# Moving a layer norm's running sums and other elementwise work off GpSimd

## The chip, the cores and the metric

The kernel runs on one core of one Trainium2 chip. The metric is the device time of one execution in microseconds (us); for a kernel that was run several times it is the median of the runs. The core's engines work side by side and wait for each other through semaphores: TensorE (PE, matrix products; its weight loads are listed apart as PEld), VectorE (DVE, elementwise work), ScalarE (ACT, one-input functions), GpSimd (POOL, elementwise work here) and SyncE (SP, which issues the transfers). Operands lie in the on-chip memory SBUF; products are accumulated in PSUM.

## The reference

The kernel computes a small encoder trunk: two layers over 512 tokens of 1024 features, fp32 in and out. Each layer is three sub-layers, each followed by a layer norm:

```python
for i in range(DEPTH):                       # DEPTH = 2
    mods = (cond @ ada_w[i] + ada_b[i]).reshape(b, N_SUB, 3, D_MODEL)
    gate = lambda s: (1 + mods[:, s, 2])[:, None, :]
    y = swiglu(modulate(x, mods[:, 0]), ffn_w_gate[i, 0], ffn_w_up[i, 0], ffn_w_down[i, 0])
    x = layer_norm(ALPHA * x + 0.5 * gate(0) * y, ln_g[i, 0], ln_b[i, 0])
    u = modulate(x, mods[:, 1])
    y = mamba2_bidir(u, ...) if i % 2 == 0 else diff_attention(u, ...)
    x = layer_norm(ALPHA * x + gate(1) * y, ln_g[i, 1], ln_b[i, 1])
    y = swiglu(modulate(x, mods[:, 2]), ffn_w_gate[i, 1], ffn_w_up[i, 1], ffn_w_down[i, 1])
    x = layer_norm(ALPHA * x + 0.5 * gate(2) * y, ln_g[i, 2], ln_b[i, 2])
```

`modulate` is x * (1 + scale) + shift, with scale and shift columns of `mods`; ALPHA is 4 ** 0.25. So the program is: FFN (n=0), a Mamba mixer (n=1), FFN (n=2), FFN (n=3), attention (n=4), FFN (n=5), with a layer norm behind each.

## The kernel before

Everything is kept transposed: the 1024 features are 8 tiles of 128 partitions, with the 512 tokens along the free axis. The residual `res` is 8 such tiles of 128x512. A product in fp32 accuracy is made of three fast products: a weight w is split into a high part `wh` (rounded by ACT) and a low part `wl = w - wh` (subtracted by DVE), an activation likewise into `uh` and `ul`, and `mm3` (line 162) issues wh·uh, wh·ul and wl·uh. Weights stream through a ring of four load buffers `raw`, loaded by SP (line 93). The first units of a sub-layer are split in two halves of 512 columns, whose parts are named `wah` (ACT, line 110) and `wal` (line 112); in the program's first units both `wal` halves are on DVE, afterwards the first half is on GpSimd and the second on DVE.

Beside the products runs the stream of the modulation: `ada_unit` (line 180) loads 512 KB of `ada_w` into the same ring and multiplies and accumulates it with the condition vector on DVE, 144 times in all.

**The startup loop** (lines 1027 and on) runs over the 8 feature tiles d. For each it makes two modulation units, two columns shift and scale (line 193, DVE), from them `uh` and `uf` (line 1045, ACT), `ul = uf - uh` (line 1047, GpSimd for d = 0, DVE for the others), scales the residual tile by ALPHA in place (line 1051, GpSimd) and splits one weight unit (lines 110 and 112, for d = 6 and 7 lines 119 and 120). Order is forced in two places: the `wah` and `wal` of a unit are made to come behind `uh` and `ul` of their tile.

**The down projection and the layer norm.** A sub-layer's last product is made unit by unit, unit d giving output tile d. `add_res` (line 371, DVE) adds it, gated, from PSUM into the residual, and `LN.feed` follows: ACT squares the tile (line 288), and two running sums over the tiles d are kept, `sc` of the values (line 292) and `ss` of the squares (line 293). For the tiles that are fed whole both sums are on GpSimd. The last KEEP tiles (4 in an FFN, 6 behind the mixer and the attention) are fed in two halves of 256 tokens; there `sc` is on DVE and `ss` on GpSimd, but for the very last tile, whose `ss` is on DVE too.

Before the first feed, `LN.start` takes a rough mean from tile 0 (ACT line 271, PE line 272, ACT line 274: `m0`) and subtracts it from all 8 residual tiles (line 277): tiles 0 to 5 on DVE, 6 and 7 on GpSimd. Once a half is complete, `stats` takes the mean of `sc` by a product with a constant matrix (line 299, PE), the sums of `sc` and `ss` per token (line 303, PE), a few small DVE steps (lines 308 to 313), a power on GpSimd (line 317) and a broadcast on PE (line 249); DVE subtracts the mean (line 321), and `normalize` multiplies (line 347, DVE) and makes the next sub-layer's `uh` and `ul` (line 349 ACT, line 350 DVE).

Four accumulators of 512 columns (`acc`) take turns, so a product whose accumulator `add_res` has not emptied waits for DVE.

**What sets the order.** A scheduler puts each engine's instructions in an order from the data they need; on an engine they then run strictly one after another. Work with no hurry is kept in a list `later`: in all sub-layers but the first the scaling of the residual waits there.

Of the kernel before, what the change touches and what calls it, by code (L numbers as in the profile page):

```python
# [17 lines left out]
KT = D // P  # L18
# [28 lines left out]
def hybrid_trunk(tc, xT, cb, par, cst, adaw, wgu, wdn0, wdn1, wdn2, wdt, win, wso, wqk, wv, wao, dist_in, dtp, lam_in, out):  # L47
# [47 lines left out]

    extra = [None]
    behind = []
    first_split = [True]
    first_ln = [None]
    turn = [0]  # L100

    def split(raw, where=None):

        n = raw.shape[-1]
        if where == "a":
            hi, lo = [], []
            for o in range(0, n, T):
                r = raw[:, o : o + T]
                h, l = big(F32R, "wah"), big(F32R, "wal")
                x = nc.scalar.activation(h, r, AF.Copy)  # L110
                eng = nc.vector if first_split[0] or o else nc.gpsimd
                y = eng.tensor_tensor(out=l, in0=r, in1=h.bitcast(F32), op=ALU.subtract)  # L112
                for a, b in zip((x, y), behind):
                    tc.add_manual_dep(a.ins, b.ins.name, NOSYNC, reason="inputs before weights")
                hi.append(h)
                lo.append(l)
            return [(hi[c // T][:, c % T : c % T + P], lo[c // T][:, c % T : c % T + P]) for c in range(0, n, P)]
        hi, lo = ring()
        nc.scalar.activation(hi[:, :n], raw, AF.Copy)  # L119
        nc.vector.tensor_tensor(out=lo[:, :n], in0=raw, in1=hi[:, :n].bitcast(F32), op=ALU.subtract)  # L120
        return Unit(hi, lo, n)
# [138 lines left out]
    class LN:  # L260
# [6 lines left out]
        def start(self):  # L267

            pm = acc("ln")
            z0 = tp.tile([P, T], F32R, tag="t", name="z0")  # L270
            nc.scalar.activation(z0, res[0], AF.Copy)
            nc.tensor.matmul(pm, lhsT=onesn, rhs=z0, start=True, stop=True)
            m0 = ap.tile([P, T], F32, tag="l", name="m0", bufs=3)
            nc.scalar.activation(m0, pm, AF.Copy)
            for d in range(KT):
                eng = nc.gpsimd if d >= 6 else nc.vector
                eng.tensor_tensor(out=res[d], in0=res[d], in1=m0, op=ALU.subtract)  # L277
            self.sc = ap.tile([P, T], F32, tag="l", name="sc", bufs=3)
            self.ss = ap.tile([P, T], F32, tag="l", name="ss", bufs=3)

        def feed(self, d, a, b, late=False):
            z = res[d][:, a:b]
            if d == 0:
                self.start()
                nc.scalar.activation(self.ss[:, a:b], z, AF.Square)
                return
            sq = sp.tile([P, T], F32, tag="sq", name="sq")
            nc.scalar.activation(sq[:, a:b], z, AF.Square)
            c0 = res[0] if d == 1 else self.sc
            e0 = nc.vector if late else nc.gpsimd  # L290
            e1 = nc.vector if late and d == KT - 1 else nc.gpsimd
            e0.tensor_tensor(out=self.sc[:, a:b], in0=c0[:, a:b], in1=z, op=ALU.add)
            e1.tensor_tensor(out=self.ss[:, a:b], in0=self.ss[:, a:b], in1=sq[:, a:b], op=ALU.add)

        def stats(self, a, b):
            n, m = self.n, (b - a) // P
# [91 lines left out]
    def down_units(n, u, units, last, KEEP=4):  # L388


        ln = LN(n) if last else None
        keep = []
        for ld in units:
            for d, w in ld():
                if last and d >= KT - KEEP:
                    keep.append((d, w))
                    continue
                pd = acc()
                proj(pd, w, u)
                add_res(d, pd, n, 0, T)  # L400
                if last:
                    ln.feed(d, 0, T)
            yield
        if last:
            rbs = []
            for a, b in HALVES:
                for d, w in keep:
                    pd = acc()
                    proj(pd, w, u, cols=((a, b),))
                    add_res(d, pd, n, a, b)  # L410
                    ln.feed(d, a, b, late=True)
                if rbs:
                    ln.normalize(*HALVES[0], rbs[0])
                rbs.append(ln.stats(a, b))
            ln.normalize(*HALVES[1], rbs[1])
            next_u[0] = ln.u
            ln.residual()
# [616 lines left out]
    for d in range(KT):  # L1034
# [8 lines left out]
        hl = tuple(ap.tile([P, T], F32R, tag="u", name=x, bufs=2 * KT) for x in ("uh", "ul"))  # L1043
        for o in (hl[0], uf):
            x = nc.scalar.activation(o, res[d], AF.Identity, bias=shift[0][:, d : d + 1], scale=onep[0][:, d : d + 1])
        eng = nc.gpsimd if d == 0 else nc.vector
        y = eng.tensor_tensor(out=hl[1], in0=uf, in1=hl[0].bitcast(F32), op=ALU.subtract)  # L1047
        behind[:] = (x, y) if d else (x,)
        first_ln[0] = y
        up.append(hl)  # L1050
        nc.gpsimd.tensor_scalar(out=res[d], in0=res[d], scalar1=ALPHA, scalar2=None, op0=ALU.mult)
        ks.append(split(load(wgu[0, d // 2, d % 2]), "a" if d < 6 else None))
        behind.clear()
    nc.sync.dma_start(csts, cst[:, : 2 * P].rearrange("p (j q) -> p j q", j=2))
    first_split[0] = False
    behind.clear()
    next_u[0] = up
    st0 = ada_stream(0, range(16, 72))
# [111 lines left out]
```

## Time and profile before

| | |
|---|---|
| runs | 2229.15, 2225.82, 2225.81 us; median 2225.82 us |
| profiled execution | 2227.95 us, of which the span of the trace is 2226.2 us |
| busy: PE, DVE, ACT, POOL | 2161.8, 1697.3, 1055.2, 273.4 us |
| startup loop | 0 to about 62 us |
| layer norms n = 0 to 5, from the first whole-tile feed on | about 350–402, 806–862, 1163–1215, 1525–1580, 1826–1862, 2177–2226 us |
| mean granted TensorE clock | 0.991 of full speed |

A row of a timeline gives the start in us, how long it took, engine, line, operation, the tiles written and read, the shape, and in square brackets the idle time of that engine just before it with what ended it. A row of a group gives line, engine, operation, tiles, shape and count, then the sum of busy time in us and the mean in ns, then the idle time in front of the group. A row of a window gives the window, its length and for PE, PEld, DVE, ACT and POOL the busy time with the number of instructions, then the granted clock, the transfer engines' busy share and GB/s. Instructions of one engine overlap by some tens of ns at their ends, so the price of one in a row of many is the distance of two starts, a little less than its listed duration.

### The profile page before, as it was taken

To read this page: it belongs to the slowest core of one execution; us is meant where nothing else is said; L and a number is where in the kernel's file an instruction comes from. 1 tells how busy PE (TensorE), PEld (TensorE's weight loads), DVE (VectorE), ACT (ScalarE), POOL (GpSimd) and SP (SyncE) were. 2 spreads that over 40 slices of the span, in tenths; PEclk is the share of its full clock that TensorE was granted. 3 is DMA by queue.
4 is the path that set the end of the run, shared out by engine and by line. 5 is a ranking of instruction groups with operands and counts; after the bars stand their busy time and mean duration, and the time that the engine had idled before them with its cause. 6 is when DMAs were issued, how large, how long until landed. Compare 5 with 4: busy or idle time off the path is not lost.

```text
span 2226.2 us, 33653 instructions
## 1 busy us (share of the span) xinstructions
PE 2161.8 (97%) x13030; PEld 1862.6 (84%) x13030; DVE 1697.3 (76%) x2850; ACT 1055.2 (47%) x1758; POOL 273.4 (12%) x332
## 2 busy tenths in 40 slices
PE   7999999999999989999999999999999999999998
PEld 5788888866777679889898989899877778989897
DVE  6865568556766689989888998897766679959696
ACT  4422234757656537434355534344755556425253
POOL 2000003035332330000003000003000012000003
PEclk9999999999999999999999999999999999999999
DMA  8865562375445423545542273733211122323231
GB/s 300 283 210 175 181 200 80 96 184 150 136 132 156 119 70 107 193 156 184 166 133 92 92 253 103 238 106 122 68 57 52 53 67 67 115 75 116 84 117 46
DMA packets 88545, 296.97 MB, mean 133 GB/s; under 512 B 9536, under 2 KB 12992, under 8 KB 88384
## 3 DMA queue, kind: packets, MB, share of 16 engines
q1 hardware_dynamic: 88384, 294.81, 41.8%
q8 instruction: 102, 1.67, 0.3%
q14 instruction: 59, 0.48, 0.1%
HBM read 289.53 MB, written 5.24 MB: 132 GB/s over the span
## 4 chain that ended last, share of the span: by engine, by line
PE 48%; DVE 9%; issue 4%; ACT 3%; DMA 2%; POOL 1%; POOLq 0%; ACTq 0%; DVEq 0%; SPq 0%
PE acc L162 38%; PE mid L162 6%; DVE wl L120 1%; DMA raw<-in_wdn 1%; PE mid L938 1%; DVE raw L464 1%; PE ln L162 1%; DVE wl L455 1%; DVE raw L180 1%; DVE lo L150 1%; PE ln L249 1%; DMA raw<-in_adaw 1%; ACT wh L119 1%; DVE resid L277 1%; DVE resid L371 0%
## 5 line engine op out<-in xcount | busy, mean ns | idle before, releaser
L162 PE MATMUL acc<-hi,wh 128*128 128x512 f32 (+1 forms) x1488 | 506.0, 341 | 9.8 <-DVE resid L371 6.7
L162 PE MATMUL acc<-hi,wl 128*128 128x512 f32 (+1 forms) x1488 | 505.9, 340 | 1.1 <-DVE wl L455 1.1
L162 PE MATMUL acc<-lo,wh 128*128 128x512 f32 (+1 forms) x1488 | 504.9, 339 | 0.0
L162 PE MATMUL acc<-uh,wh 128*128 128x512 f32 (+1 forms) x1256 | 441.6, 352 | 0.3 <-ACT wh L119 0.3
L162 PE MATMUL acc<-ul,wh 128*128 128x512 f32 (+1 forms) x1256 | 439.5, 350 | 0.2 <-DVE ul L1047 0.2
L162 PE MATMUL acc<-uh,wl 128*128 128x512 f32 (+1 forms) x1256 | 438.2, 349 | 0.8 <-DVE wl L120 0.8
L119 ACT ACTIVATE wh<-raw 128x1024 fp32r<-128x1024 f32 (+1 forms) x234 | 238.6, 1025 | 392.3 <-PE acc L162 199.1
L120 DVE TENSOR_TENSOR wl<-raw,wh 128x1024 fp32r<-128x1024 f32 (+1 forms) x234 | 281.2, 1202 | 81.1 <-ACT wh L119 71.3
L162 PEld LDWEIGHTS acc<-hi,wh 128*128 128x128 f32 x1488 | 283.8, 191 | 46.2 <-DVE resid L371 6.5
L162 PEld LDWEIGHTS acc<-hi,wl 128*128 128x128 f32 x1488 | 284.1, 191 | 32.2 <-DVE wl L455 1.5
L162 PEld LDWEIGHTS acc<-lo,wh 128*128 128x128 f32 x1488 | 283.9, 191 | 31.0 <-DVE lo L150 1.0
L162 PEld LDWEIGHTS acc<-uh,wh 128*128 128x128 f32 x1256 | 237.4, 189 | 40.2 <-issue 9.2
L454 ACT ACTIVATE wh<-raw 128x1024 fp32r<-128x1024 f32 x162 | 170.8, 1059 | 207.5 <-DVE raw L464 105.2
L162 PEld LDWEIGHTS acc<-uh,wl 128*128 128x128 f32 x1256 | 237.6, 189 | 35.0 <-issue 3.9
L162 PEld LDWEIGHTS acc<-ul,wh 128*128 128x128 f32 x1256 | 237.8, 189 | 33.7 <-issue 4.4
L180 DVE SCALAR_TENSOR_TENSOR raw<-raw,cond 128x1024 f32<-128x1024 f32 x144 | 176.9, 1235 | 55.8 <-DMA raw<-in_adaw 55.4
L455 DVE TENSOR_TENSOR wl<-raw,wh 128x1024 fp32r<-128x1024 f32 x162 | 196.9, 1219 | 27.1 <-ACT wh L454 26.1
L371 DVE SCALAR_TENSOR_TENSOR resid<-acc,gv,resid 128x512 f32<-128x512 f32 (+1 forms) x172 | 113.0, 659 | 78.5 <-PE acc L162 78.2
L464 DVE TENSOR_TENSOR raw<-raw 128x512 f32<-128x512 f32 x216 | 148.1, 689 | 4.4
L112 POOL TENSOR_TENSOR wal<-raw,wah 128x512 fp32r<-128x512 f32 x13 | 19.7, 1517 | 951.7 <-ACT wah L110 655.5
L162 PE MATMUL mid<-uh,wh 128*128 128x256 f32 (+2 forms) x332 | 94.7, 286 | 0.9 <-DVE up L496 0.9
L162 PE MATMUL mid<-uh,wl 128*128 128x256 f32 (+2 forms) x332 | 93.9, 283 | 0.0
(269 smaller groups left out, 3824.8 us busy)
## 6 DMA issues: line engine op xcount, KB each, us to landing
raw<-in_wgu SPq DMA_DIRECT2D x176, 512.0 KB, 3.9
raw<-in_adaw SPq DMA_DIRECT2D x144, 512.0 KB, 4.6
raw<-in_wdn SPq DMA_DIRECT2D x64, 448.0 KB, 3.7
raw<-in_win SPq DMA_DIRECT2D x40, 512.0 KB, 3.6
raw<-in_wdn SPq DMA_DIRECT2D x32, 512.0 KB, 4.5
rw<-scr SPq DMA_DIRECT2D x32, 512.0 KB, 5.4
ch<-scr SPq DMA_DIRECT2D x32, 256.0 KB, 3.5
raw<-in_wso SPq DMA_DIRECT2D x16, 512.0 KB, 3.5
```

Source lines behind the costliest of these rows:

```text
L119: nc.scalar.activation(hi[:, :n], raw, AF.Copy)
L120: nc.vector.tensor_tensor(out=lo[:, :n], in0=raw, in1=hi[:, :n].bitcast(F32), op=ALU.subtract)
L150: y = nc.vector.tensor_tensor(out=lo, in0=src, in1=hi.bitcast(F32), op=ALU.subtract)
L162: last = nc.tensor.matmul(o, lhsT=a, rhs=b, start=start and j == 0, stop=j == n - 1, skip_group_check=not start)
L180: nc.vector.scalar_tensor_tensor(out=raw, in0=raw, scalar=1.0, in1=cond, op0=ALU.mult, op1=ALU.mult, accum_out=mods[l][:, j : j + 1],)
L249: nc.tensor.matmul(o[:, j * P : (j + 1) * P], lhsT=cols[:, j : j + 1].broadcast_to([P, P]), rhs=ident, start=True, stop=True)
L277: eng.tensor_tensor(out=res[d], in0=res[d], in1=m0, op=ALU.subtract)
L371: nc.vector.scalar_tensor_tensor(out=res[d][:, a:b], in0=pd[:, a:b], scalar=gvec[n][:, d : d + 1], in1=res[d][:, a:b], op0=ALU.mult, op1=A ...
L454: nc.scalar.activation(x[0], r, AF.Copy)
L455: nc.vector.tensor_tensor(out=x[1], in0=r, in1=x[0].bitcast(F32), op=ALU.subtract)
L464: nc.vector.tensor_tensor(out=o, in0=x, in1=y, op=ALU.add)
L938: nc.tensor.matmul(ss[m], lhsT=a[r, c], rhs=b[r, :], start=j == 0, stop=j == 2)
```

## The change

All running sums, all eight subtractions of the rough mean, all `wal` halves and the `ul` of tile 0 are issued to DVE; the scaling of the residual by ALPHA in the startup loop is an ACT instruction that is put on the list `later`. GpSimd keeps the small powers (lines 243 and 317) and two steps of the mixer (lines 763 and 777).

```diff
@@ split
                 x = nc.scalar.activation(h, r, AF.Copy)
-                eng = nc.vector if first_split[0] or o else nc.gpsimd
-                y = eng.tensor_tensor(out=l, in0=r, in1=h.bitcast(F32), op=ALU.subtract)
+                y = nc.vector.tensor_tensor(out=l, in0=r, in1=h.bitcast(F32), op=ALU.subtract)
@@ LN.start
             for d in range(KT):
-                eng = nc.gpsimd if d >= 6 else nc.vector
-                eng.tensor_tensor(out=res[d], in0=res[d], in1=m0, op=ALU.subtract)
+                nc.vector.tensor_tensor(out=res[d], in0=res[d], in1=m0, op=ALU.subtract)
@@ LN.feed
-        def feed(self, d, a, b, late=False):
+        def feed(self, d, a, b):
...
             c0 = res[0] if d == 1 else self.sc
-            e0 = nc.vector if late else nc.gpsimd
-            e1 = nc.vector if late and d == KT - 1 else nc.gpsimd
-            e0.tensor_tensor(out=self.sc[:, a:b], in0=c0[:, a:b], in1=z, op=ALU.add)
-            e1.tensor_tensor(out=self.ss[:, a:b], in0=self.ss[:, a:b], in1=sq[:, a:b], op=ALU.add)
+            nc.vector.tensor_tensor(out=self.sc[:, a:b], in0=c0[:, a:b], in1=z, op=ALU.add)
+            nc.vector.tensor_tensor(out=self.ss[:, a:b], in0=self.ss[:, a:b], in1=sq[:, a:b], op=ALU.add)
@@ the startup loop
-        eng = nc.gpsimd if d == 0 else nc.vector
-        y = eng.tensor_tensor(out=hl[1], in0=uf, in1=hl[0].bitcast(F32), op=ALU.subtract)
+        y = nc.vector.tensor_tensor(out=hl[1], in0=uf, in1=hl[0].bitcast(F32), op=ALU.subtract)
...
-        nc.gpsimd.tensor_scalar(out=res[d], in0=res[d], scalar1=ALPHA, scalar2=None, op0=ALU.mult)
+        later.append(lambda d=d: nc.scalar.activation(res[d], res[d], AF.Copy, scale=ALPHA))
```

The line numbers fall by 1 to 6 with it: line 112 is line 110 afterwards, 110 is 109, 180 is 178, 277 is 274, 292 and 293 are 287 and 288, 299 and 303 are 294 and 298, 371 is 366, 1045 and 1047 are 1040 and 1041, and the scaling, 1051, is 1045.

Three places show how the instructions stand. The first is ACT in the startup loop, at the first two tiles (`uh`, `uf`: the modulated input and its high part; `wah`: a weight's high part). Before:

```order
L1045 ACTIVATE uh<-resid,sh_93,sc_94 128x512
L1045 ACTIVATE uf<-resid,sh_93,sc_94 128x512
L110 ACTIVATE wah<-raw 128x512 x2
L1045 ACTIVATE uh<-resid,sh_93,sc_94 128x512
L1045 ACTIVATE uf<-resid,sh_93,sc_94 128x512
```

Now:

```order
L1040 ACTIVATE uh<-resid,sh_93,sc_94 128x512
L1040 ACTIVATE uf<-resid,sh_93,sc_94 128x512
L109 ACTIVATE wah<-raw 128x512
L1045 ACTIVATE resid<-resid 128x512
L109 ACTIVATE wah<-raw 128x512
L1040 ACTIVATE uh<-resid,sh_93,sc_94 128x512
L1040 ACTIVATE uf<-resid,sh_93,sc_94 128x512
```

Though it is put on the list `later`, the scaling stands inside the loop, between the two high parts of each weight unit.

The second place is DVE in the norm behind the FFN n = 2, from the subtraction of the rough mean on (`acc`: the accumulators that line 371 empties; `wl`, `wal`: low weight parts; `raw`, `mods1`: a modulation unit). Before:

```order
L277 TENSOR_TENSOR resid_88<-resid_88,m0_10724 128x512 x6
L371 SCALAR_TENSOR_TENSOR resid_88<-acc_10743,gv2_2543,resid_88 128x512
L120 TENSOR_TENSOR wl_10857<-raw_10854,wh_10856 128x896
L112 TENSOR_TENSOR wal_11253<-raw_11246,wah_11252 128x512
L371 SCALAR_TENSOR_TENSOR resid_88<-acc_10776,gv2_2543,resid_88 128x512
L180 SCALAR_TENSOR_TENSOR raw_11380,mods1_87<-raw_11380,cond_73 128x1024
L120 TENSOR_TENSOR wl_11386<-raw_11383,wh_11385 128x1024
L180 SCALAR_TENSOR_TENSOR raw_11513,mods1_87<-raw_11513,cond_73 128x1024
L371 SCALAR_TENSOR_TENSOR resid_88<-acc_10809,gv2_2543,resid_88 128x512
```

Now:

```order
L274 TENSOR_TENSOR resid_88<-resid_88,m0_10724 128x512 x8
L366 SCALAR_TENSOR_TENSOR resid_88<-acc_10743,gv2_2543,resid_88 128x512
L366 SCALAR_TENSOR_TENSOR resid_88<-acc_10776,gv2_2543,resid_88 128x512
L287 TENSOR_TENSOR sc_10734<-resid_88 128x512
L288 TENSOR_TENSOR ss_10735<-ss_10735,sq_10766 128x512
L287 TENSOR_TENSOR sc_10734<-sc_10734,resid_88 128x512
L288 TENSOR_TENSOR ss_10735<-ss_10735,sq_10799 128x512
L118 TENSOR_TENSOR wl_10857<-raw_10854,wh_10856 128x896
L110 TENSOR_TENSOR wal_11249<-raw_11246,wah_11248 128x512
L366 SCALAR_TENSOR_TENSOR resid_88<-acc_10809,gv2_2543,resid_88 128x512
```

The subtractions are eight, the sums of the whole tiles stand on DVE in pairs, and the weight split and the modulation units come behind them.

The third place is PE in the norm behind the mixer (n = 1), at the statistics of its second half (`acc_7141`: the last down unit; `acc_7315` and the others with `uh_7159`: the next FFN's first products; `sc`, `ss`: the running sums). Before:

```order
L162 MATMUL acc_7141<-hi_6773,wl_6915 128x256
L162 MATMUL acc_7315<-uh_7159,wah_7287 128x256
L162 MATMUL acc_7364<-uh_7159,wah_7297 128x256
L162 MATMUL acc_7448<-uh_7159,wah_7307 128x256
L162 MATMUL acc_7497<-uh_7159,wh_7444 128x256
L299 MATMUL mid_7216<-sc_6879,onesd_89 128x256
L303 MATMUL ln_7215<-invd_78,sc_6879 128x1 x2
L303 MATMUL ln_7215<-invd_78,ss_6880 128x1 x2
L162 MATMUL acc_7315<-ul_7160,wah_7287 128x256
```

Now:

```order
L160 MATMUL acc_7141<-hi_6773,wl_6915 128x256
L294 MATMUL mid_7216<-sc_6879,onesd_89 128x256
L298 MATMUL ln_7215<-invd_78,sc_6879 128x1 x2
L298 MATMUL ln_7215<-invd_78,ss_6880 128x1 x2
L160 MATMUL acc_7315<-uh_7159,wah_7287 128x256
L160 MATMUL acc_7315<-ul_7160,wah_7287 128x256
L160 MATMUL acc_7315<-uh_7159,wal_7288 128x256
```

The four products of the next FFN that stood ahead of the statistics stand behind them. The norm behind the attention (n = 4) moves in the same way.

4 lines of the change are left out of this document (1 added, 3 removed).

## The prediction

> **What bounds the kernel now.** The page's first part comes first, then the waits of PE.
>
> ```profile
> PE 2161.8 (97%) x13030; PEld 1862.6 (84%) x13030; DVE 1697.3 (76%) x2850; ACT 1055.2 (47%) x1758; POOL 273.4 (12%) x332
> PE acc L162 <- ACT wah L110: 11.5, 1, 11.5
> PE acc L162 <- DVE resid L371: 6.7, 3, 3.1
> PE mid L299 <- DVE sc L292: 6.3, 4, 3.6
> ```
>
> PE fills 97% of the span of 2226.2 us; 64.4 us are left in which it stands still. An edit of elementwise work can only shorten these and the stretches in which PE runs at a lower clock. 11.5 us are the start (one wait); of the rest the largest are DVE's `add_res` and DVE's running sum in the layer norms. So the stages in which PE waits for DVE have to be found and priced one by one; the total of DVE says little.
>
> **What moves.** The groups by shape, first of GpSimd (busy us, mean ns), then the like ones of DVE:
>
> ```profile
> L293 POOL TENSOR_TENSOR ss<-ss,sq 128x256 f32<-128x256 f32 x44 | 34.1, 775 | 42.1 <-ACT sq L288 40.5
> L293 POOL TENSOR_TENSOR ss<-ss,sq 128x512 f32<-128x512 f32 x14 | 20.9, 1494 | 0.0
> L277 POOL TENSOR_TENSOR resid<-resid,m 128x512 f32<-128x512 f32 x12 | 20.5, 1731 | 318.1 <-ACT m L274 316.6 <-PE acc L162 1.5
> L112 POOL TENSOR_TENSOR wal<-raw,wah 128x512 fp32r<-128x512 f32 x13 | 19.7, 1517 | 951.7 <-ACT wah L110 655.5 <-PE ln L272 295.5 <-DVE wal L112 0.6
> L292 POOL TENSOR_TENSOR sc<-resid 128x512 f32<-128x512 f32 x6 | 12.8, 2137 | 18.6 <-DVE resid L371 18.6
> L292 POOL TENSOR_TENSOR sc<-sc,resid 128x512 f32<-128x512 f32 x8 | 11.8, 1474 | 1.9 <-DVE resid L371 1.9
> L277 DVE TENSOR_TENSOR resid<-resid,m 128x512 f32<-128x512 f32 x36 | 38.6, 1138 | 4.1 <-ACT m L274 4.1
> L112 DVE TENSOR_TENSOR wal<-raw,wah 128x512 fp32r<-128x512 f32 x25 | 26.8, 1074 | 3.2 <-ACT wah L110 3.2
> L292 DVE TENSOR_TENSOR sc<-sc,resid 128x256 f32<-128x256 f32 x56 | 32.2, 575 | 6.8 <-POOL sc L292 6.3
> L321 DVE TENSOR_TENSOR resid<-resid,mid 128x256 f32<-128x256 f32 x96 | 36.0, 412 | 1.8 <-PE mid L299 1.8
> ```
>
> The last row is DVE's price for 256 columns without GpSimd beside it, 412 ns; for 512 it is 680 (the `wal` at 33.50, in the next fence). In a row of several I take 0.33 and 0.60 us, the distance of two starts (33.50 to 34.10; for 256 less the same 0.08). Taken over are 40 instructions of 512 columns from the L293, L277 and L292 rows (14 + 12 + 6 + 8), 13 `wal` and one `ul`: 54 x 0.60 + 44 x 0.33 = 47 us. In return DVE's own operations with both inputs in SBUF, which before stood beside GpSimd, become cheaper: (1138 − 680) x 36 = 16.5, (1074 − 680) x 25 = 9.9, (575 − 412) x 56 = 9.1, 35 us in three rows, some more in the weight splits beside them. DVE ends about 5 to 12 us busier, so at about 1705; ACT takes 8 scalings of 0.6. The total is nearly even, so where the work lies decides.
>
> **A. The startup loop, −3 us.** One round (d = 3), and the rows that stand around it:
>
> ```profile
> 28.97 0.16 DVE L193 SCALAR_TENSOR_TENSOR sc<-mods,pars 128x1 f32<-128x1 f32 x1
> 29.17 0.82 ACT L1045 ACTIVATE uh<-resid,sh,sc 128x512 fp32r<-128x512 f32 x1 [3.82 <-DVE sc L193]
> 30.72 0.69 DVE L1047 TENSOR_TENSOR ul<-uf,uh 128x512 fp32r<-128x512 f32 x1 [1.59 <-ACT uf L1045]
> 30.77 1.99 POOL L1051 TENSOR_SCALAR resid<-resid 128x512 f32<-128x512 f32 x1 [4.39 <-ACT uf L1045]
> 31.33 1.10 DVE L112 TENSOR_TENSOR wal<-raw,wah 128x512 fp32r<-128x512 f32 x1
> 32.36 1.21 DVE L180 SCALAR_TENSOR_TENSOR raw<-raw,cond 128x1024 f32<-128x1024 f32 x1
> 33.50 0.68 DVE L112 TENSOR_TENSOR wal<-raw,wah 128x512 fp32r<-128x512 f32 x1
> 34.10 1.21 DVE L180 SCALAR_TENSOR_TENSOR raw<-raw,cond 128x1024 f32<-128x1024 f32 x1
> 35.36 0.16 DVE L193 SCALAR_TENSOR_TENSOR sc<-mods,pars 128x1 f32<-128x1 f32 x1
> 31.91 0.40 PE L162 MATMUL acc<-uh,wah 128*128 128x512 f32 x1
> 32.48 0.49 PE L162 MATMUL acc<-uh,wal 128*128 128x512 f32 x1 [0.17 <-DVE wal L112]
> 32.82 0.39 PE L162 MATMUL acc<-ul,wah 128*128 128x512 f32 x1
> 49.74 1.23 DVE L180 SCALAR_TENSOR_TENSOR raw<-raw,cond 128x1024 f32<-128x1024 f32 x1 [0.32 <-DMA raw<-in_adaw]
> ```
>
> DVE's round is 35.36 − 28.97 = 6.39 us. The `wal` beside GpSimd's scaling takes 32.36 − 31.33 = 1.03, the one without it 0.60: 0.43 a round, in five rounds 2.1. In the first round DVE has a `wal` pair, `ul` and the scaling of GpSimd at once, worth about another 1 us, and the two last tiles 0.4 more: DVE's loop could end 3.5 us sooner. PE follows only as far as it waits: starts at 31.91, 32.48 and 32.82 instead of 0.23 apart, 0.45 lost in a round, with like losses in the other rounds, about 4 us in all. Against it stand the transfers, for which DVE waits already at 49.74. Bounds −0.5 and −4; I take −3, near the rows of DVE. ACT's scaling lies between two `wah` and so 0.6 before the second of these; its `wal` stands one modulation unit later on DVE, and ACT has 3.82 us idle in a round. Without that cover it would cost up to 0.6 x 8 = 4.8.
>
> **B. The norm behind FFN n = 2, −4.5 us.**
>
> ```profile
> 1168.01 3.52 POOL L277 TENSOR_TENSOR resid<-resid,m 128x512 f32<-128x512 f32 x2 [0.88 <-ACT m L274]
> 1168.61 6.99 DVE L277 TENSOR_TENSOR resid<-resid,m 128x512 f32<-128x512 f32 x6
> 1186.49 0.36 PE L162 MATMUL acc<-hi,wh 128*128 128x256 f32 x1 [0.62 <-DVE resid L371]
> 1194.06 1.19 PE L299 MATMUL mid<-sc,onesd 128*128 128x256 f32 x2 [3.65 <-DVE sc L292]
> 1196.00:1198.00 2.00, 2.00 (x10) 2.00 (x11) 1.22 (x7) 0.00 (x0) 0.17 (x1) 0.50 0.00 0
> ```
>
> Six subtractions take 6.99 us on DVE beside two on GpSimd; all eight alone are 8 x 0.60 = 4.8. What follows on DVE is late by that, runs beside GpSimd's sums, and PE stands 3.65 us before the statistics. From there the clock is 0.50 until about 1200.7: of 6.7 us half, 3.3, are lost. So 0.62 + 3.65 + 3.3 = 7.6 us are there. Afterwards DVE has per half unit an `add_res` (0.40), two sums (0.66) and for most a modulation unit or a split (1.14): 2.2 us, against about 2.5 of PE. DVE keeps up, but behind the last product it still has these 2.2, of which PE covers about 1 with ten products of the next unit: a wait of up to 1.3. I take 7.6 − 1.3 and half of the clock's loss as staying: −4.5. Bounds −3 (the clock falls all the same) and −6.5.
>
> **C and D. The norms behind mixer and attention, −1.5 and −2.5 us.**
>
> ```profile
> 816.89 0.39 PE L162 MATMUL acc<-hi,wh 128*128 128x256 f32 x1 [2.92 <-DVE resid L371]
> 818.00:820.00 2.00, 2.00 (x12) 1.95 (x12) 1.58 (x3) 0.42 (x1) 2.00 (x2) 0.57 0.51 141
> 822.34 0.47 DVE L371 SCALAR_TENSOR_TENSOR resid<-acc,gv,resid 128x256 f32<-128x256 f32 x1
> 822.73 0.56 DVE L292 TENSOR_TENSOR sc<-sc,resid 128x256 f32<-128x256 f32 x1
> 828.00:830.00 2.00, 1.73 (x11) 1.43 (x9) 2.00 (x7) 0.00 (x0) 1.45 (x2) 0.63 0.01 4
> 825.81 0.67 PE L299 MATMUL mid<-sc,onesd 128*128 128x256 f32 x2 [0.74 <-DVE sc L292]
> 1838.97 0.58 PE L162 MATMUL acc<-hi,wh 128*128 128x256 f32 x1 [3.14 <-DVE resid L371]
> ```
>
> Here PE waits 2.92 and 3.14 us for the first `add_res` behind the subtractions, and runs for 3.3 us at 0.57. Eight subtractions of 0.60 instead of 6.3 us bring this `add_res` 1.4 sooner; but behind it a split and two whole sums (1.14 + 1.2) now stand ahead of the next ones, which gives back about 1.2. What is won is the clock (about 1.7) and the 0.74 before the statistics. In the second half the statistics of PE stand directly behind the last product, with no `uh` products ahead; DVE must first do `add_res` and two sums for one or two half units, 1.06 each (0.39, as 822.34 to 822.73, and twice 0.33): 1.1 to 2.1 lost, and about 1.2 when the next products start before ACT has more than one `uh` ready (an estimate: ACT made `uh` and `uf` at 0.72 each in the startup, two such tiles of half the width and their like). Sum for C: −0.2 − 1.7 − 0.7 − 1.6 (a second such stretch of slow clock, from 828) + 2.1 + 1.2 − 0.6 (waits that fall away) = −1.5, bounds −4 and +2. D has the same rows and one more gain: a slowed `wal` ahead of the rough mean, 1.1: −2.5, bounds −5 and +1.
>
> The clock fell behind a wait of 2.92 us, and again (0.63 from 828) behind 0.74 and smaller ones; so I count waits of 1 to 2 us as able to cost it. By the Trainium skill, "TensorE: Matmul & The Clock Gate", section "Part 1: The HAM clock gate", it falls after an idle window of about 3.4 us. By that, what is left of the waits would cost no clock in B, C and D, the rival "more" below; the 0.63 at 828 speaks against it.
>
> **E. The other norms, 0.** There PE has no gap though DVE is slowed in the same way:
>
> ```profile
> 360.00:380.00 20.00, 20.00 (x147) 18.86 (x146) 15.16 (x28) 5.13 (x10) 13.95 (x11) 1.00 0.32 106
> ```
>
> DVE is busy 15.2 of 20 us; some 8 us more for a norm, half of it given back, still fit, so PE's work hides them. Without that cover it would be up to 4 us a norm.
>
> **Sum:** −3 − 4.5 − 1.5 − 2.5 = −11.5 us against the profiled execution of 2227.95, so 2216.4. That execution lies 2.1 over the median of 2225.82; the forecast for the median is 2225.82 − 11.5 = 2214.3.
>
> **The rivals.**
> *No change.* Each gain at its poor end: A −0.5, B −3, C +2, D +1 make −0.5, so 2225.3. For it speaks that DVE takes on 47 us and gets back little over 35; against it that B alone has 7.6 us to win. Chance 0.10. The Trainium skill, "Perfetto Trace Analysis", section "Optimizing Scalar/DVE Operations", says that shifting work between GpSimd and DVE might not help, since they share a read port; the trace agrees in that DVE's 1138 ns stand against 680 without GpSimd, and by that sentence the way back would be even too.
> *Slower.* In the norms of mixer and attention the late statistics become the bound: 2.1 + 1.2 lost and, once PE's wait is near 3 us, a stretch at 0.57 like that at 818, 1.7: +5 in each, while the first half gains nothing and the startup stands on its transfers. With B at −3 this is +7, 2233. It decides once the last half unit's chain leaves PE idle for about 3 us. For it speaks the order of PE, against it that DVE is then behind by two units at most. Chance 0.08.
> *Only the norms.* The transfers hold the startup as it is, 0 instead of −3, and D is as C: 2218.5. Chance 0.17.
> *More.* The waits that are left in B, C and D are too short to lower the clock, and the late statistics are covered: −3 − 6.5 − 4 − 5 = −18.5, 2207. Chance 0.15.
> *The change doesn't do what it says:* the scaling, meant for later, stands in the startup loop on ACT. It is in the sum of A already; if it sat on the path, A would be +1.8 and the time 2219. It is counted with "only the norms".
>
> The forecast itself has 0.50. What a measurement of this kernel tells from no change is about 0.2%, 4.5 us. Faster by more than that are the forecast, "more" and "only the norms", 0.82; same 0.10; slower 0.08. The range runs from "more", 2206, to just short of no change, 2224.
>
> **What would show it.** GpSimd at about 136 us busy (273.4 less the six rows' 119.8, eight scalings of 2.0 and one `ul`) and DVE near 1705; the subtraction at about 0.68 us each, 48 of them; DVE's startup round at 5.96 us, with PE's waits of 0.17 gone; no wait over 1.5 us before the statistics of n = 2, and no window of clock 0.50 behind it; PE standing still for some 55 us instead of 64.4. A wait of 2 us or more before the second statistics of n = 1 and n = 4 would show the rival. The forecast is wrong if DVE's sums make `add_res` late in the norms of E, where I put nothing.

## The result, and the profile after

The changed kernel took 2213.81 us (median of 4 runs, 2210.46 to 2218.04), the kernel before beside it 2227.49 us (4 runs, 2225.81 to 2229.16): a ratio of 0.994, 95% interval 0.9919 to 0.996. Timed once more on the chip of the experiments it was 2211.43 against 2223.2 us, 0.995 (0.9938 to 0.9962), 11.8 us faster. The forecast was 2214.3 us, 11.5 us faster. The total came out as forecast; three of its four terms didn't.

The page's first part and the waits of PE in the changed kernel:

```profile
PE 2156.0 (97%) x13030; PEld 1858.7 (84%) x13030; DVE 1701.8 (77%) x2948; ACT 1059.4 (48%) x1766; POOL 136.2 (6%) x226
PE acc L160 <- ACT wah L109: 11.6, 2, 11.4
PE mid L294 <- DVE sc L287: 6.4, 4, 2.5
PE acc L160 <- DVE resid L366: 5.3, 4, 1.5
```

GpSimd has lost half of its work, 137 us, and DVE is busier by 4.5 us only, though it executes 98 instructions more. The groups by shape show why:

```profile
L274 DVE TENSOR_TENSOR resid<-resid,m 128x512 f32<-128x512 f32 x48 | 29.4, 684 | 1.5 <-ACT m L272 1.5
L110 DVE TENSOR_TENSOR wal<-raw,wah 128x512 fp32r<-128x512 f32 x38 | 25.6, 684 | 1.3 <-ACT wah L109 1.2
L287 DVE TENSOR_TENSOR sc<-sc,resid 128x256 f32<-128x256 f32 x56 | 23.4, 418 | 0.4
L288 DVE TENSOR_TENSOR ss<-ss,sq 128x256 f32<-128x256 f32 x56 | 23.4, 419 | 1.8 <-ACT sq L285 0.6
```

48 subtractions now cost less (29.4 us) than 36 did (38.6), and 38 low parts less (25.6) than 25 (26.8). PE's busy time fell by 5.8 us at the same number of products. What PE waits for the sums, however, is still 6.4 us. It stands elsewhere.

To see where, the start of the same product of PE (there are 13030 in each trace, in nearly the same order) is compared with its start in the first trace of before. This is worked out from the timelines; a minus is earlier:

| change over the stage, us | before, second trace | changed | changed, second trace | forecast |
|---|---|---|---|---|
| A: startup, 0–66 | −0.6 | −2.3 | −2.4 | −3 |
| B: norm n = 2, 1150–1225 | +0.1 | −7.2 | −7.8 | −4.5 |
| C: norm n = 1, 790–960 | −1.2 | +0.5 | −1.0 | −1.5 |
| D: norm n = 4, 1815–2150 | +0.1 | −0.1 | +0.2 | −2.5 |
| E: norms n = 0, 3 and 5 | +0.1 | −0.6 | −0.9 | 0 |
| all between them | −3.1 | −3.8 | −5.1 | – |

So B gives most of it, A its share, C and D nothing. The last row is no part of the change's reasons: two traces of the same kernel before differ there by 3.1 us.

**The startup.** One round of the changed loop, on DVE and ACT, and a later wait of DVE:

```profile
27.02 0.16 DVE L191 SCALAR_TENSOR_TENSOR sc<-mods,pars 128x1 f32<-128x1 f32 x1
29.16 0.61 ACT L1045 ACTIVATE resid<-resid 128x512 f32<-128x512 f32 x1
29.38 0.68 DVE L110 TENSOR_TENSOR wal<-raw,wah 128x512 fp32r<-128x512 f32 x1
29.98 1.22 DVE L178 SCALAR_TENSOR_TENSOR raw<-raw,cond 128x1024 f32<-128x1024 f32 x1
32.99 0.16 DVE L191 SCALAR_TENSOR_TENSOR sc<-mods,pars 128x1 f32<-128x1 f32 x1
43.07 1.23 DVE L178 SCALAR_TENSOR_TENSOR raw<-raw,cond 128x1024 f32<-128x1024 f32 x1 [0.95 <-DMA raw<-in_adaw]
```

The round is 32.99 − 27.02 = 5.97 us instead of 6.39, `wal` 0.60 from start to start instead of 1.03, and the scaling lies on ACT beside it. From 43 us on DVE waits for transfers, 0.95 here, which takes back a part.

**The norm n = 2.** DVE's last modulation unit ahead of the first statistics, PE at these statistics, and the two windows behind them:

```profile
1183.75 1.23 DVE L178 SCALAR_TENSOR_TENSOR raw<-raw,cond 128x1024 f32<-128x1024 f32 x1 [0.57 <-DMA raw<-in_adaw]
1185.37 0.70 PE L294 MATMUL mid<-sc,onesd 128*128 128x256 f32 x2 [0.57 <-DVE sc L287]
1186.00:1188.00 2.00, 2.00 (x20) 2.00 (x19) 1.53 (x7) 0.76 (x1) 0.00 (x0) 1.00 0.81 260
1188.00:1190.00 2.00, 1.97 (x17) 1.76 (x16) 1.90 (x6) 0.31 (x2) 0.70 (x1) 1.00 0.00 0
```

The wait is 0.57 instead of 3.65 us, the one of 0.62 for `add_res` is gone, and the clock stays at 1.00 where it was 0.50. Even the 0.57 is not the sums' own time: DVE's modulation unit just ahead of them waited 0.57 us for its transfer. In the second trace it waited for none, and neither did PE.

**The norms n = 1 and n = 4.** PE's waits in both, DVE's last sum of n = 1, the clock behind it, and the stretch of n = 4 in which the lead is lost:

```profile
810.62 0.39 PE L160 MATMUL acc<-hi,wh 128*128 128x256 f32 x1 [1.53 <-DVE resid L366]
813.44 0.36 PE L160 MATMUL acc<-hi,wh 128*128 128x256 f32 x1 [1.13 <-DVE resid L366]
829.23 0.41 DVE L287 TENSOR_TENSOR sc<-sc,resid 128x256 f32<-128x256 f32 x1
829.70 0.70 PE L294 MATMUL mid<-sc,onesd 128*128 128x256 f32 x2 [2.45 <-DVE sc L287]
832.00:836.00 4.00, 4.00 (x20) 4.00 (x21) 3.69 (x14) 4.00 (x9) 0.49 (x1) 0.50 0.01 2
1840.91 0.70 PE L294 MATMUL mid<-sc,onesd 128*128 128x256 f32 x2 [2.10 <-DVE sc L287]
1842.00:1846.00 4.00, 3.86 (x28) 3.34 (x28) 3.69 (x13) 4.00 (x9) 0.00 (x0) 1.00 0.00 0
1846.00:1850.00 4.00, 3.53 (x31) 3.33 (x29) 3.70 (x14) 3.55 (x8) 0.90 (x1) 1.00 0.00 2
1850.00:1854.00 4.00, 3.35 (x25) 2.81 (x23) 3.84 (x13) 3.30 (x7) 0.00 (x0) 1.00 0.00 0
1858.00:1862.00 4.00, 4.00 (x36) 4.00 (x35) 2.56 (x5) 3.97 (x7) 0.00 (x0) 1.00 0.90 277
```

The first half does what was forecast: 1.53 where 2.92 stood, and a new wait of 1.13. At the last product ahead of the second statistics PE is ahead of the first trace of before, by 9.5 us in n = 1 and 18.2 in n = 4 (4.9 and 13.9 at the norms' start). Then it waits for DVE's last sums, 2.45 and 2.10 us. In the kernel before, the same stretch from the last product to the statistics takes 1.24 and 1.74 us, with four products in it, so the lead is still 8.3 and 17.9 us at the statistics. Most of it is lost behind them: at the end of the norms 4.0 and 14.4 us are left. In n = 1 half clock follows the wait. In n = 4 it doesn't, and the lead is lost all the same: from 1846 to 1854 PE is idle for 1.1 of 8 us and gets 56 products done, against 36 in 4 us from 1858 on, while DVE is busy for 7.5 of 8. In the second trace of the changed kernel a stretch of half clock of 3.4 us lies in this place of n = 4, and the loss behind the statistics is 3.5 us as in the first, so here the clock isn't what costs it.

**The other norms.** The window that answers to the one shown of n = 0:

```profile
358.00:378.00 20.00, 19.98 (x148) 18.86 (x147) 15.78 (x36) 4.16 (x9) 0.70 (x1) 1.00 0.33 106
```

DVE does the added work and PE still has no gap.

### The profile page after: what moved, and what is told of

It reads as the page before. It is cut to its first block, busy times and chain, and to the rows that moved or that the text cites. A ratio compares the mean times of both kernels' runs of the same rounds, so it can differ in the third digit from the quotient of the medians.

```text
span 2213.0 us, 33554 instructions
## 1 busy us (share of the span) xinstructions
PE 2156.0 (97%) x13030; PEld 1858.7 (84%) x13030; DVE 1701.8 (77%) x2948; ACT 1059.4 (48%) x1766; POOL 136.2 (6%) x226
## 4 chain that ended last, share of the span: by engine, by line
PE 78%; DVE 10%; ACT 4%; DMA 3%; issue 3%; POOL 1%; POOLq 0%; ACTq 0%; SPq 0%; DVEq 0%
PE acc L160 64%; PE mid L160 6%; PE mid L783 2%; DMA raw<-in_adaw 1%; DVE raw L178 1%; PE mid L933 1%; DMA raw<-in_wdn 1%; DVE wl L118 1%; DVE raw L459 1%; PE ln L160 1%; DVE wl L450 1%; PE ln L247 1%; POOL E L772 1%; DVE lo L148 1%; PE ln L731 1%
## 5 line engine op out<-in xcount | busy, mean ns | idle before, releaser
L312 POOL TENSOR_TENSOR rr<-vr,mhalf 128x2 f32<-128x2 f32 x12 | 8.8, 732 | 1545.2 <-DVE vr L308 1545.2
```

## The experiments

All are timed beside the kernel before. "n = 2" and so on below mean the change of PE's lead over that stage, as in the table above.

**The startup undone.** The scaling and the first `ul` go back to GpSimd.

```diff
-        y = nc.vector.tensor_tensor(out=hl[1], in0=uf, in1=hl[0].bitcast(F32), op=ALU.subtract)
+        eng = nc.gpsimd if d == 0 else nc.vector
+        y = eng.tensor_tensor(out=hl[1], in0=uf, in1=hl[0].bitcast(F32), op=ALU.subtract)
...
-        later.append(lambda d=d: nc.scalar.activation(res[d], res[d], AF.Copy, scale=ALPHA))
+        nc.gpsimd.tensor_scalar(out=res[d], in0=res[d], scalar1=ALPHA, scalar2=None, op0=ALU.mult)
```

> The changed kernel with the startup loop as before (the scaling of the residual and the ul of tile 0 on GpSimd), everything else changed. Theory (the startup gives about 2.3 us of the gain, by the step of 2.26 us that PE's products show between 0 and 62 us, and nothing later depends on it): about 2.3 us slower than the changed kernel, DVE's round back at 6.38 us. Rival (what the startup wins is given back by waits for transfers): within 0.5 us of the changed kernel.

2214.8 us, ratio to before 0.9966 (0.9953 to 0.9979); the changed kernel has 0.995, or 2211.43 us, so about 3.4 us slower. The startup's change of lead is +0.2 instead of −2.3, DVE's round is 6.39 us again (28.84 to 35.23), and n = 2 keeps its −7.8. The startup is worth what the traces say, and nothing later hangs on it. In all eleven traces with the changed startup it lies between −2.3 and −4.3. The changed kernel's DVE waited 0.95 us for a transfer at 43 us, the kernel with the squares on GpSimd (−4.1, below) for none from 36 to 56 us: that differs from one execution to the next.

**The norms n = 1 and n = 4 undone.** There sums, subtractions and the `wal` of the next sub-layer are as before.

```diff
+                eng = nc.gpsimd if d >= 6 and self.n in (1, 4) else nc.vector
...
+            e0 = nc.gpsimd if self.n in (1, 4) and not late else nc.vector
+            e1 = nc.gpsimd if self.n in (1, 4) and not (late and d == KT - 1) else nc.vector
```

> The changed kernel with the norms n = 1 and n = 4 (sums, subtractions of the rough mean, low weight parts of the next sub-layer) as before. Theory (these two norms win nothing: the first half's gain is given back by late statistics and a fully busy DVE): within 2 us of the changed kernel, either way. Forecast on record (terms C and D): 4 us slower than the changed kernel. Rival (the late statistics cost net): 2 to 4 us faster than the changed kernel.

2211.67 us, ratio 0.9949 (0.9936 to 0.9961), no different from the changed kernel. n = 1 shows +0.5 and n = 4 +0.1, as the changed kernel does. In these two norms the change is worth nothing either way; terms C and D of the forecast, 4 us together, did not come.

**The FFN norms undone.** The same for n = 0, 2, 3 and 5.

> The changed kernel with the norms of the four FFNs as before. Theory (nearly all of the gain of the norms lies in the norm n = 2): 7 to 9 us slower than the changed kernel, with the wait of about 3.6 us before the statistics of n = 2 and a stretch of half clock behind it back. Forecast on record (term B): 4.5 us slower.

2218.88 us, ratio 0.9984 (0.9975 to 0.9993), 7.5 us over the changed kernel by the two medians. n = 2 has a change of +0.2, against −7.8. The row of PE is that of before:

```profile
1188.89 1.07 PE L300 MATMUL mid<-sc,onesd 128*128 128x256 f32 x2 [3.65 <-DVE sc L293]
```

**Squares on GpSimd in n = 1 and n = 4.** Only the running sum of squares of the half tiles goes back.

```diff
-            nc.vector.tensor_tensor(out=self.ss[:, a:b], in0=self.ss[:, a:b], in1=sq[:, a:b], op=ALU.add)
+            e1 = nc.gpsimd if self.n in (1, 4) and b - a < T and d < KT - 1 else nc.vector
+            e1.tensor_tensor(out=self.ss[:, a:b], in0=self.ss[:, a:b], in1=sq[:, a:b], op=ALU.add)
```

> The changed kernel, but in the norms n = 1 and n = 4 the running sum of squares of the half tiles (but the last) is on GpSimd, as before; the order of PE puts four products of the next FFN ahead of the second statistics again. Theory (the statistics come late there because DVE makes both sums): the waits of 2.45 and 2.10 us before them fall under 1 us, the first normalisation starts no later, and the kernel is 2 to 5 us faster than the changed one. Rival (GpSimd beside DVE slows DVE's own sums and subtractions by as much as it takes off): within 1 us of the changed kernel.

2205.18 us (2203.34 to 2206.66), ratio 0.9921 (0.9909 to 0.9933): 18.3 us faster than the kernel before and 6 us faster than the changed one, the best of all. n = 1 is −3.1, n = 4 −2.5. PE's waits in n = 1 up to the second statistics, DVE's last sum ahead of these, and a window from that stretch:

```profile
806.64 0.39 PE L160 MATMUL acc<-hi,wh 128*128 128x256 f32 x1 [1.53 <-DVE resid L367]
809.46 0.36 PE L160 MATMUL acc<-hi,wh 128*128 128x256 f32 x1 [1.13 <-DVE resid L367]
815.11 0.70 PE L295 MATMUL mid<-sc,onesd 128*128 128x256 f32 x2 [0.50 <-DVE sc L287]
818.43 0.71 PE L247 MATMUL ln<-csts,rr 128*128 128x128 f32 x4 [0.30 <-POOL rr L313]
824.72 0.62 PE L160 MATMUL acc<-uh,wah 128*128 128x256 f32 x3 [0.44 <-ACT uh L345]
825.05 0.42 DVE L287 TENSOR_TENSOR sc<-sc,resid 128x256 f32<-128x256 f32 x1
826.00:830.00 4.00, 4.00 (x35) 3.97 (x34) 3.85 (x13) 3.75 (x8) 0.00 (x0) 1.00 0.02 4
```

No wait stands before the second statistics any more (the next one is 0.41 us, for GpSimd's power, at 832), and the clock stays at 1.00. Two things differ there at once. Four products of the next FFN stand ahead of these statistics again, as in the kernel before, and DVE's last sum ends 1.2 us after the last down product instead of 2.4. The two waits of `add_res` in the first half are as in the changed kernel. GpSimd does slow DVE: the sums of 256 columns take 457 ns in the mean, against 418, 2 us over all of them. That is less than the 20 sums taken off.

**The subtraction spread out.** The last kernel, but in n = 1 and n = 4 only three subtractions of the rough mean are issued at first, and the others each two tiles ahead of their use.

```diff
-            for d in range(KT):
-                nc.vector.tensor_tensor(out=res[d], in0=res[d], in1=m0, op=ALU.subtract)
+            self.m0 = m0
+            for d in range(3 if self.n in (1, 4) else KT):
+                self.sub(d)
...
+            if self.n in (1, 4) and a == 0 and d + 2 < KT:
+                self.sub(d + 2)
```

> The kernel with the squares on GpSimd in n = 1 and 4, and there the subtraction of the rough mean is issued for three tiles at first and for each further tile when the tile two before it is fed, so that add_res needn't wait for eight subtractions in a row. Theory (the two waits of 1.53 and 1.13 us in the first half of both norms come from the row of eight): they fall under 0.5 us each, 2 to 4 us faster than with the squares on GpSimd alone. Rival (DVE has too much work in this half, the wait only moves to the statistics): within 1 us.

2211.14 us, ratio 0.9948 (0.9933 to 0.9962): 6 us slower, neither of the two expectations.

```profile
810.64 0.36 PE L160 MATMUL acc<-hi,wh 128*128 128x256 f32 x1 [0.50 <-DVE resid L373]
813.95 0.39 PE L160 MATMUL acc<-hi,wh 128*128 128x256 f32 x1 [0.21 <-DVE resid L373]
827.35 0.61 DVE L291 TENSOR_TENSOR sc<-sc,resid 128x256 f32<-128x256 f32 x1
828.02 0.70 PE L301 MATMUL mid<-sc,onesd 128*128 128x256 f32 x2 [2.11 <-DVE sc L291]
1838.81 0.70 PE L301 MATMUL mid<-sc,onesd 128*128 128x256 f32 x2 [2.05 <-DVE sc L291]
```

The first waits do shrink, to 0.50 and 0.21 us in n = 1; in n = 4 one of 1.20 and one of 0.21 remain. But the scheduler now puts the second statistics directly behind the last down unit again, as in the changed kernel, and the waits of 2.1 us are back, with the squares on GpSimd. PE's lead over the first trace of before, worked out from the timelines, shows where the gain goes (n = 1, n = 4):

| lead, us | norm's start | last product ahead of the second statistics | at these statistics | norm's end |
|---|---|---|---|---|
| changed | 4.9, 13.9 | 9.5, 18.2 | 8.3, 17.9 | 4.0, 14.4 |
| squares on GpSimd | 8.9, 22.5 | 12.5, 25.8 | 12.5, 26.3 | 10.9, 25.1 |
| subtraction spread | 5.3, 15.2 | 10.9, 20.3 | 10.0, 20.0 | 4.5, 17.2 |

Up to the last product the spread subtraction wins 5.6 and 5.1 us, against 3.6 and 3.3 with the squares alone: that much of the theory holds. From there to the norm's end it loses 6.4 and 3.1 us, against 1.6 and 0.7, which is more than it had won, so the rival's mechanism, by which the wait only moves to the statistics, is the one that came.

It would be easy to put all of this down to the place of the statistics in PE's order, since the waits of 2.0 us and more come only where they stand directly behind the last product. The rows of DVE's last sum say that this is at most a part. It ends 2.4 us after the last down product in the changed kernel, 2.05 here and 1.2 with the squares alone and in the kernel before (n = 1). So with the squares alone the statistics could start 1.2 us sooner because the sums were ready sooner, and the order filled about 0.8 us of what was left with products. The order alone wasn't tried. Of the difference between the two traces 2.6 us lie in the two norms, 1.3 in the startup and 3.6 between the stages, which is of the kind that differs between two traces of one kernel.

**The subtraction alone, the sums alone, the low parts alone.** Three kernels undo one part each: the subtraction of tiles 6 and 7, or the sums, both in the four FFN norms, or the first `wal` halves everywhere.

```diff
+                eng = nc.gpsimd if d >= 6 and self.n in (0, 2, 3, 5) else nc.vector
```

> The changed kernel with only the subtraction of the rough mean in the four FFN norms as before (tiles 6 and 7 on GpSimd). Theory (what delays DVE at n = 2 is the sums on GpSimd, which run beside it for 15 us): at most 2 us slower than the changed kernel, the wait before the statistics of n = 2 under 1.5 us. Rival (the slow subtraction of 6.99 us starts the delay): the wait of 3 us and the half clock come back, 5 to 8 us slower.

```diff
+            late = b - a < T
+            e0 = nc.gpsimd if self.n in (0, 2, 3, 5) and not late else nc.vector
+            e1 = nc.gpsimd if self.n in (0, 2, 3, 5) and not (late and d == KT - 1) else nc.vector
```

> The changed kernel with only the running sums of the four FFN norms as before (whole tiles and the squares on GpSimd). Theory (the sums do it): the wait before the statistics of n = 2 is 2 us or more, with a slow stretch behind it, 5 to 8 us slower than the changed kernel. Rival (the subtraction does it): at most 2 us slower.

```diff
+                eng = nc.gpsimd if o == 0 and later_split[0] else nc.vector
```

> The changed kernel with only the first halves of the low weight parts (wal) on GpSimd after the startup, as before. Theory (13 of them, 6 beside the norms n = 1, 2 and 4 ahead of the rough mean, matter little alone): 0 to 2 us slower than the changed kernel. Rival (they are what the undone pair of subtraction and sums lacked to the full loss at n = 2): 3 us slower or more, with the loss at n = 2.

2214.53, 2214.97 and 2215.05 us, ratios 0.9964, 0.9963 and 0.9971 (each within 0.0012). The first two are 3.1 and 3.5 us slower than the changed kernel, which was timed beside them; the third was timed with another group of runs, and is 3.6 us slower by the medians and 4.7 by the ratios. n = 2 gives −5.5, −5.6 and −5.1 instead of −7.8. The statistics' rows, in this order:

```profile
1185.14 0.70 PE L295 MATMUL mid<-sc,onesd 128*128 128x256 f32 x2 [1.23 <-DVE sc L288]
```

```profile
1186.65 0.67 PE L297 MATMUL mid<-sc,onesd 128*128 128x256 f32 x2 [2.15 <-DVE sc L290]
```

```profile
1182.84 0.70 PE L296 MATMUL mid<-sc,onesd 128*128 128x256 f32 x2 [1.12 <-DVE sc L289]
```

I had looked for one culprit, and there is none. The 5 to 8 us that the expectations gave to the sums or to the subtraction came from neither, and the low parts, expected to cost 2 us at most, cost as much as the others, as their rival had it. Measured from the changed kernel's second trace, each part undone costs 2.2 to 2.7 us at n = 2; the three together make 7.2, and undoing all of them 8.0. These are single traces, and the seven traces in which nothing of n = 2 was undone (the one with the fills, below, among them) lie between −7.2 and −7.9, so that the costs are known to some 0.7 us. With a wait of 1.12 or 1.23 the clock went to 0.50 behind the statistics, with 2.15 it did not: in these three traces the loss is of like size either way.

**GpSimd busy for nothing.** The changed kernel, and in the FFN norms GpSimd adds the rough mean to itself twelve times, into a tile that nobody reads; in a second kernel it fills that tile with zeros 24 times instead, behind one addition of 4 columns.

```diff
+            if self.n in (0, 2, 3, 5):
+                for _ in range(12):
+                    nc.gpsimd.tensor_tensor(out=scratch, in0=m0, in1=m0, op=ALU.add)
```

> The changed kernel, and in the four FFN norms GpSimd makes twelve additions of 128x512 into a tile that nobody reads, from the rough mean on; nothing waits for them but GpSimd's own power of the statistics. Theory (in the norm n = 2 the kernel before lost its time because GpSimd's reads beside DVE slow DVE): DVE's subtractions of the rough mean go from 0.68 to 1 us or more in these norms, the wait before the statistics of n = 2 is 1.5 us or more, 3 to 8 us slower than the changed kernel. Rival (DVE waited for GpSimd's sums and not beside them): the subtractions stay under 0.8 us, within 1 us of the changed kernel.

```diff
+                nc.gpsimd.tensor_tensor(out=scratch[:, :4], in0=m0[:, :4], in1=m0[:, :4], op=ALU.add)
+                for _ in range(24):
+                    nc.gpsimd.memset(scratch, 0.0)
```

> The same with 24 fills of the tile with zeros in place of the additions: GpSimd is as busy, but reads nothing. Theory (it is the reads): DVE's subtractions stay at 0.68 us, within 1 us of the changed kernel. Rival (any work of GpSimd in SBUF slows DVE): they rise as with the additions.

With the additions 2241.54 us, ratio 1.0081 (1.0064 to 1.0099): 30 us slower than the changed kernel, far more than the 3 to 8 expected, and slower than before. With the fills 2213.36 us, ratio 0.9952 (0.9934 to 0.9971): no difference. Nothing of DVE's waits for these additions, and GpSimd stands idle for 6 us or more before each of its powers, so it is no dependence. The rows of n = 2, first with additions:

```profile
1168.07 22.47 POOL L278 TENSOR_TENSOR scratch<-m 128x512 f32<-128x512 f32 x12 [328.50 <-ACT m L273]
1168.21 4.90 DVE L275 TENSOR_TENSOR resid<-resid,m 128x512 f32<-128x512 f32 x8
1173.03 1.40 DVE L370 SCALAR_TENSOR_TENSOR resid<-acc,gv,resid 128x512 f32<-128x512 f32 x2
1175.60 1.52 DVE L292 TENSOR_TENSOR ss<-ss,sq 128x512 f32<-128x512 f32 x1
1177.05 1.53 DVE L291 TENSOR_TENSOR sc<-sc,resid 128x512 f32<-128x512 f32 x1
1197.79 1.22 PE L298 MATMUL mid<-sc,onesd 128*128 128x256 f32 x2 [7.23 <-DVE sc L291]
```

and with fills:

```profile
1161.41 5.09 POOL L277 TENSOR_TENSOR scratch<-m 128x4 f32<-128x4 f32 x1 [325.82 <-ACT m L273]
1161.55 4.90 DVE L275 TENSOR_TENSOR resid<-resid,m 128x512 f32<-128x512 f32 x8
1166.56 13.96 POOL L279 MEMSET scratch<- 128x512 f32 x24
1168.90 0.69 DVE L292 TENSOR_TENSOR sc<-sc,resid 128x512 f32<-128x512 f32 x1
1184.39 0.70 PE L299 MATMUL mid<-sc,onesd 128*128 128x256 f32 x2 [0.46 <-DVE sc L292]
```

Beside GpSimd's additions one of DVE's sums takes 1.45 us (1175.60 to 1177.05) instead of 0.60; beside its fills 0.69 is listed, the undisturbed value. The subtractions, by which the expectation wanted to see it, slowed to that price in n = 0 and n = 5 only; in n = 2 and n = 3 they kept 0.60 (last section). `add_res`, which reads one input from PSUM, keeps its pace (two in 1.40 us, as in the changed kernel). The other FFN norms, where the changed kernel has −0.6 to −0.9 between them, show +18.4 with the additions: PE's work hides only so much there. By the Trainium skill, "SBUF — State Buffer", section "Who interferes with whom", a DVE instruction with two SBUF inputs contends with a GpSimd instruction that reads SBUF, not with one that only writes; both kernels agree.

**The kernels again.** The changed kernel and the kernel before once more.

> The changed kernel once more, timed beside the kernel before, on the chip of the following runs. Theory (the gain is the change's): about 11 to 13 us faster than the kernel before, between the run with the FFN norms undone and the run with the squares on GpSimd; in the trace the norm n = 2 again without a slow stretch. Rival (part of the 13 us is how often the clock fell in the two profiled executions): 8 to 10 us faster.

> The kernel before, profiled a second time. Every trace of the changed kernels is 2.4 us ahead between 410 and 520 us, at the mixer's start, whichever part is undone. Theory (the first profile of before had one more stretch of half clock there by chance): the second profile of before is ahead of the first there too, by 1.7 to 2.5 us. Rival (the change does it, by the weight parts at the mixer's start): the second profile agrees with the first there within 0.5 us. In the norm n = 2 it should show the wait of 3.6 us again.

The changed kernel took 2211.43 us, 11.8 us less than the kernel before beside it: the theory. The second trace of before, 2223.39 us, is 4.6 us shorter than the first; 2.7 us of it, a little over the 1.7 to 2.5 expected, lie between 410 and 520 us, where every changed kernel had seemed to gain. So at least most of that gain was in the first trace of before, not in the change. In n = 2 the second trace repeats the first:

```profile
1189.69 0.67 PE L299 MATMUL mid<-sc,onesd 128*128 128x256 f32 x2 [3.66 <-DVE sc L292]
```

## Why the prediction was right, and where it wasn't

**The total** was right by cancelling errors: B gave 3 us more than its term, C and D 4 us less together. Of the 13.5 us between the two traces first compared, some 3 were no gain of the change but lie in the first trace of before; what moves the stretches between the norms by up to 3 us from one execution to the next stays open, beyond the steps of the clock (last section).

**The prices** held. DVE's 680 ns, now on every subtraction and low part, the 47 us taken over against 35 and some given back, GpSimd at 136 us: DVE rose by 4.5 us, just under the 5 to 12 forecast. PE stands still for 57.0 and 55.5 us in the two traces, where some 55 were forecast. That the cause is GpSimd's reads of SBUF was read from rows then; the pair of additions and fills shows it.

**A** was right: round 5.97 (5.96), PE's small waits gone, transfers as what remains. −3 against −2.3 and −2.4, and a mean of −3.4 over all eleven traces. The rival by which the scaling on ACT would sit on the path fell: it lies where it was said to lie.

**B** was right in its mechanism and too small in size, outside its own bound of −6.5. The term that was mis-sized is what would remain: a wait of up to 1.3 us and half of the clock's loss. Measured were 0.57 us in the first trace, none in the second, and no loss of clock. The chain of DVE behind the last product was counted rightly, 2.2 us: it took 2.0 in the second trace, and 2.7 in the first with the wait of 0.57 for a transfer in it. What failed is its cover, put at 1 us with ten products of the next unit: eighteen stand there and cover 2.2.

**C and D** failed at one step, "1.1 to 2.1 lost, and about 1.2 when the next products start". The waits of the first half came as forecast (1.53 and 1.13), and PE won 4.6 and 4.4 us up to the last product. The second statistics waited 2.45 and 2.10, near the upper figure or over it, but only 1.2 and 0.4 more than the same stretch takes in the kernel before. It is behind them that the term was too small: 4.3 and 3.5 us were lost there instead of about 1.2. In n = 1 half clock lay in it, which the sum had taken off as gone; in n = 4 the loss is the same with such a stretch and without, while DVE was busy for 7.5 of 8 us. The rival "slower" had this place and this mechanism right; its price of 5 us a norm was too high by the first half's gain, which it had left out. With the squares on GpSimd the losses behind the statistics fall to 1.6 and 1.2 us, and the two norms give 3.1 and 2.5 us, more than C and D had asked for together. So it is the sums of squares on DVE that took the gain there; how much of it goes by DVE's load and how much by the order of PE, which moved with it, stays open.

**E** held: under 1 us in three norms.

Two of the rivals' sums are a little off: "only the norms" adds up to 2218.3 us, and "more" to 2207.3, while the range starts at 2206. Neither changes anything here.

## What to carry to other kernels

A slower engine beside DVE is no free help when both read SBUF: price it by the rows of DVE's own instructions, with it beside them and without, before counting what it takes off. What such a move is worth stands in the stages where the matrix engine waits; the same edit gave 7.8 us in one norm and nothing in two others, and giving back just one sum in those two won 6 us more. After a move, look at both engines at the place where one waits: when the last sum ends on DVE, and what stands ahead of the waiting product on PE. Here the first made 1.2 us of the difference, and the second some 0.8.

## What the hardware did that was not expected

When GpSimd's addition and DVE's row of eight subtractions start within 0.14 us of each other, either may win. In n = 2, with additions and with fills, the eight took their undisturbed 4.90 us. GpSimd's first addition stood beside the whole row: it took 5.94 us, and with the fills, where it has 4 columns only, 5.09 us. In n = 0 it went the other way, with GpSimd 0.13 us ahead again:

```profile
349.91 12.69 POOL L278 TENSOR_TENSOR scratch<-m 128x512 f32<-128x512 f32 x9 [348.84 <-ACT m L273]
350.04 11.66 DVE L275 TENSOR_TENSOR resid<-resid,m 128x512 f32<-128x512 f32 x8
```

There the eight took 11.66 us and GpSimd's additions 1.4 each. Which of the two it will be was not to be seen from the start times.

The low clock doesn't follow from the length of a wait. 2.45 us at 829.70 were followed by 0.50 for 6.8 us, 2.10 us at 1840.91 by none; in the second trace of the changed kernel the same place of n = 4 has 3.4 us of it. By the Trainium skill, "TensorE: Matmul & The Clock Gate", section "Part 1: The HAM clock gate", the clock is judged in free-running windows of about 3.4 us; the stretches in these norms last one or two such lengths, 3.41 or 6.83 us, and that a wait of one length has a stretch behind it in one trace and none in another agrees. But waits far below a whole window, 1.12 us, had one behind them.

Where PE sets the pace, a stretch of 3.41 us should cost half of it, 1.7 us (an estimate from the clock of 0.50); in n = 4, where PE waits for DVE, it cost nothing. Without the end of the span, the two traces of before have nine and seven such lengths at half clock, the two of the changed kernel six and five (one of the five in n = 4), the one with the squares on GpSimd three. By that estimate the two lengths more are 3.4 of the 4.6 us between the traces of before, and, the one in n = 4 not counted, about all of the 3.4 between those of the changed kernel. So two traces are to be compared with the clock in view.
